# Mixer D's chunk recurrence for two pairs of heads at a time, and matmuls with 64 contraction rows in place of zero-padded ones

## Chip, cores and metric

One core of one Trainium2 chip runs the whole program in one launch. The metric is the time of that launch on the device in microseconds. TensorE is called PE here, VectorE DVE, ScalarE ACT, GpSimd POOL; SP issues the DMAs.

## What is computed

Two layers of a bidirectional encoder on 256 tokens of width 2048. Cut to what matters here:

```python
u = rmsnorm(h);  z = u @ w_in            # 6528 columns for the four mixers A, B, C, D
h += concat[A(zA), B(zB), C(zC), D(zD)] @ w_out
h += relu(rmsnorm(h) @ w_up)**2 @ w_down
h += (p @ w_ple) * sigmoid(rmsnorm(h) @ w_gate)
# A: 4 heads, two maps (m) of width 64 each, softmax(q k^T/8 + bias), o0 - lam*o1
# D (RWKV-7), 8 heads of width 64, forward and backward in time:
#   decay = exp(-0.607*sigmoid(w0 + tanh(wl) @ w2));  a = sigmoid(a0 + al @ a2);  g = sigmoid(gl) @ g2
#   state = state*w_t - (state @ kk_t) b_t^T + v_t k_t^T;   y_t = state @ r_t
#   out = (groupnorm(y) + bonus) * g
```

## The kernel before

Activations lie with the channel on the partition and the 256 tokens along the free axis. Every large product streams its weights from HBM in units of 128x1024 (512 KB). `wsplit` (L140) splits each unit into a rounded part `wh` (ACT, L148) and a remainder `wl` (DVE, L150), both `float32r`; `mm2` (L166, L167) or `mm3` (L158 to L160) multiplies them with the split activations `u`, `act`, `mh`. These rows are called weight rows below: an L166 row streams 512 columns, each of the others 256. The rest of the mixers' arithmetic is in plain `float32`, and PE runs such a matmul as two passes, each a record of the trace (a transpose is one).

Mixer D has two parts. `first` (L509, for c = 0 to 3, a pair of heads each) makes decay, rate and keys of a direction d, the products `psam` (L600) and transposed keys (`psbt`, L618). `invert` (L638) inverts small triangular blocks on DVE. `second` (L662) is called for c = 1, 3, 0, 2 one after the other (L439). In it `psW` (L704, L708) joins two 32-row blocks of each inverse, and four chunk steps follow, in each of which both directions advance by one chunk of 64 tokens: `psr`/`pss` gets the keys' product with the state (L741) and, from the step before, the values' part (`v_part`, L728); DVE copies it to `R` (L744); L749 multiplies it by the inverse; DVE copies that to `ST` (L751); L759 makes the state's increment; DVE multiplies the old state by the decay (L764) and adds (L768); L774 and L779 add to the output `psy`. Groupnorm and gating follow (L783 to L798).

`mixer_a` (L891) makes the logits of a head: two query blocks qc, two maps m. The query tile `qn` holds map 0 with its lower 64 rows zero and map 1 with its upper 64 rows zero (L910 to L912), so that L929 contracts over all 128 rows. In `first` the matrices of the decay and of the rate are laid out the same way: the tile `lora` holds 128 rows per direction, of which 64 are zero (L515, L556, L561).

No order is written out by hand: a scheduler places every engine's instructions when the program is built, from data dependencies and its own costs, so the steps of `second` stand between weight rows of the products that feed mixers A, B and C. Each engine then runs its list in that order. SBUF addresses come from pools; `shift` (L84) inserts a pad.

An operand's partitions set which part of PE's array a matmul takes: rows by where its inputs lie, columns by where its output lies in PSUM. L749 and L728 take 64 rows by 64 columns (L749 from partitions 0 to 63, L728 from 64 to 127, both to columns 0 to 63); L759 and L774 take all rows and, by turns, one or the other half of the columns; L600 by turns the upper and the lower half of the rows, and all columns.

Of the kernel before, what the change touches and what calls it, by code (L numbers as in the profile page):

```python
# [16 lines left out]
P = 128  # L17
# [17 lines left out]
PCOLS = [("mixg", 16), ("mlpg", 16), ("pleg", 16), ("aq", 2), ("ak", 1), ("asub", 1), ("hl0", 4), ("hl1", 4),  # L35
# [37 lines left out]
def trunk(ctx: ExitStack, tc: tile.TileContext, xT, pT, w_in, w_out1, w_out2, w_up, w_down, w_gate, w_ple, pvec,  # L73
          rel, lam, consts, lmask, onehot, lora, lorag, cw, outT, stages=None):
# [13 lines left out]
    shift(cp, 24)  # L88
# [180 lines left out]
    for l in range(DEPTH):  # L269
# [9 lines left out]
        mh1 = op_.__enter__().tile([P, NOUT1, 2 * S], F32R, name="mh1")  # L279
# [19 lines left out]
        for k in range(NOUT1):  # L299
            load_mix(mh1[:, k], k)  # L300
# [8 lines left out]
        mh2 = K.up.tile([P, KC - NOUT1, 2 * S], F32R, tag="u1", name="mh2")  # L309
        for k in range(NOUT1, KC):  # L310
            load_mix(mh2[:, k - NOUT1], k)
# [95 lines left out]
def mixers(K):  # L407
# [31 lines left out]
    for c in (1, 3, 0, 2):  # L439
        D.second(c)  # L440
# [14 lines left out]
class MixerD:  # L455
# [30 lines left out]
    def t2(self, tag="t2", bufs=4):  # L486
        return self.K.dp.tile([P, S], F32, tag=tag, name=tag, bufs=bufs)
# [21 lines left out]
    def first(self, c, base):  # L509
# [5 lines left out]
        lo = df.tile([P, 2, 2, P], F32, tag="lora", name="lora", bufs=1)  # L515
        nc.sync.dma_start(lo, K.lora[l, c])
        lg = df.tile([P, P], F32, tag="lorag", name="lorag", bufs=2)
        nc.sync.dma_start(lg, K.lorag[l, c])
# [29 lines left out]
        ksum = t1("ks", 1)  # L548
        for d in range(2):
            sd = sp[:, d]  # L550

            pad, inc0 = (0, 1) if d == 0 else (64, 0)
            sg = df.tile([P, 4, 65], F32, tag="sg", name="sg", bufs=1)
            V.memset(sg[:, :, pad:pad + 1], 0.0)
            ps = pds("psw")
            T.matmul(ps[:, :S], lo[:, 0, d], self.wl, start=True, stop=True)  # L556
            K.sigmoid(sg[:, :, inc0:inc0 + 64], ps[:, :S].rearrange("p (a b) -> p a b", a=4),
                      bias=self.nw[:, d * 4 + c:d * 4 + c + 1])
            a = t1()
# [48 lines left out]
            for blk in range(2):  # L608
# [4 lines left out]
            BE = df.tile([P, 3, P], F32, tag="BE", name="BE", bufs=1)  # L613
            G.tensor_tensor(BE, BK[:, d:d + 3].rearrange("p j a b -> p j (a b)"),
                            EL[:, d:d + 3].unsqueeze(2).to_broadcast([P, 3, P]), ALU.mult)
            ps = pds("psbt")
            for j in range(3):
                T.transpose(ps[:, j * P:(j + 1) * P], BE[:, j], mat("ident"))  # L618
# [14 lines left out]
        T.matmul(ps[:, :S], lg, self.gl, start=True, stop=True)  # L633
# [28 lines left out]
    def second(self, c):  # L662

        K, t2, sp, xs = self.K, self.t2, self.sp.pop(c), self.xs
        if c == 0:
            sp = self.slot(c)
            for d in range(2):
                K.nc.sync.dma_start(sp[:, d], self.sscr[c, d])
        nc, l, dp = K.nc, K.l, K.dp
        V, A, G, T = nc.vector, nc.scalar, nc.gpsimd, nc.tensor  # L670
        mat, pc, pds = K.mat, K.pc, K.pds


        ST = dp.tile([P, 2, 4, 2, 64], F32, tag="ST", name="ST", bufs=1)
        for d in range(2):
            nc.sync.dma_start(ST[64:, d].rearrange("p j h v -> p j (h v)"),
                              self.vscr[c].rearrange("(j s) v -> s j v", s=64))

        def am(rows, d, h, j, a):
            o = SP_AM + h * 512 + j * P + a * 64  # L680
            return sp[rows, d, o:o + 64]

        TT = dp.tile([P, 2, 8, 64], F32, tag="lane", name="Tm", bufs=2)

        U = dp.tile([P, 8, 32], F32, tag="U32", name="U32", bufs=2)
        W = dp.tile([P, 8, 32], F32, tag="W32", name="W", bufs=1)
        G.memset(TT[0:64], 0.0)
        bs = [slice(0, 32), slice(32, 64)]

        def v8(t):  # L690
            return t.rearrange("p (a b) -> p a b", a=8)
        for d in range(2):
            lane = (d * 64 + c * 16) * 1024
            Tm = TT[:, d]

            x, y = (0, 1) if d == 0 else (1, 0)
            for t, b, w in ((U[bs[x]], x, d), (Tm[bs[0], :, bs[0]], 0, 1 - d), (Tm[bs[1], :, bs[1]], 1, 1 - d)):
                nc.sync.dma_start(t, bass.AP(xs.tensor, xs.offset + w * P * 1024 + lane + b * 8192,
                                             [[32, 32], [1024, 8], [1, 32]]))

            ps = pds("psW")
            for i in range(8):
                o = SP_AM + i * P
                T.matmul(ps[bs[y], i * 32:(i + 1) * 32], sp[bs[x], d, o + 32 * y:o + 32 * y + 32], U[bs[x], i],  # L704
                         start=True, stop=True)
            A.activation(W[bs[y]], v8(ps[bs[y], :S]), AF.Copy)
            for i in range(8):
                T.matmul(ps[bs[x], S + i * 32:S + (i + 1) * 32], W[bs[y], i], Tm[bs[y], i, bs[y]],  # L708
                         start=True, stop=True)
            V.tensor_copy(Tm[bs[x], :, bs[y]], v8(ps[bs[x], S:]))  # L710


        SS = dp.tile([P, 3, 2, P], F32, tag="SS", name="SS", bufs=1)
        G.memset(SS, 0.0)

# [3 lines left out]
        def both(ap, o, w):  # L719

            return strided(ap, o(0), [[o(1) - o(0), 2], [1, w]])

        def v_part(ps, st):
            for d in range(2):
                j = at(st, d)
                for h in range(2):
                    o = S + d * P + h * 64
                    T.matmul(ps[0:64, o:o + 64], am(slice(64, P), d, h, j, 0), ST[64:, d, j, h],  # L728
                             start=(st == 0 and d + h == 0), stop=(st == 0), skip_group_check=True)
        psr = pds("psr")  # L730
        v_part(psr, 0)
        bg = dp.tile([P, 2, S], F32, tag="bg2", name="bg2", bufs=2)
        nc.sync.dma_start(bg, self.late[c])
        psy = pds("psy")
        first = [True, True]
        for st in range(4):
            js = [at(st, d) for d in range(2)]
            if st:
                for d in range(2):
                    o = SP_KS + js[d] * P  # L740
                    T.matmul(psr[0:64, S + d * P:S + (d + 1) * P], sp[:, d, o:o + 64], SS[:, st - 1, d],  # L741
                             start=False, stop=True, skip_group_check=True)
            R = dp.tile([P, 2, P], F32, tag="R", name="R", bufs=1)
            V.tensor_copy(R[0:64], psr[0:64, S:].rearrange("p (a b) -> p a b", a=2))  # L744
            psr = pds("pss")
            for d in range(2):
                for h in range(2):
                    o = d * P + h * 64
                    T.matmul(psr[0:64, o:o + 64], TT[0:64, d, h * 4 + js[d]], R[0:64, d, h * 64:(h + 1) * 64],  # L749
                             start=(d + h == 0), stop=True, skip_group_check=True)  # L750
            V.tensor_copy(both(ST[0:64], lambda d: d * 512 + js[d] * P, P),  # L751
                          psr[0:64, :S].rearrange("p (a b) -> p a b", a=2))
            if st < 3:
                v_part(psr, st + 1)
                ps = pds("psst")
                for d in range(2):
                    o = SP_BB + (js[d] - d) * P
                    for h in range(2):
                        T.matmul(ps[HS[h], d * 64:d * 64 + 64], sp[:, d, o:o + P][:, HS[h]], ST[:, d, js[d], h],  # L759
                                 start=True, stop=True)  # L760
                pst = ps[:, :P].rearrange("p (a b) -> p a b", a=2)
                if st:
                    dec = dp.tile([P, 2, P], F32, tag="dec", name="dec", bufs=1)
                    V.tensor_tensor(dec, SS[:, st - 1], strided(sp, SP_EL + js[0], [[SP_N + js[1] - js[0], 2], [0, P]]),  # L764
                                    ALU.mult)
                for h in range(2):
                    if st:
                        V.tensor_tensor(SS[HS[h], st, :, HS[h]], dec[HS[h], :, HS[h]], pst[HS[h]], ALU.add)  # L768
                    else:
                        V.tensor_copy(SS[HS[h], st, :, HS[h]], pst[HS[h]])  # L770
# [417 lines left out]
```

## Time and profile before

| | us |
|---|---|
| median of 3 runs | 2740.97 (2737.82 to 2740.99) |
| the profiled execution | 2741.71 |
| its span, first to last instruction | 2740.0 |
| PE busy | 2688.3 (98%) |
| DVE busy | 1972.6 (72%) |
| ACT busy | 1608.3 (59%) |
| POOL busy | 77.3 (3%) |

The profiled execution lies 0.74 us above the median. Busy time counts a matmul until its modelled end, and matmuls overlap, so a row's start and the start of the next row tell what it took of PE. Mixer D of layer 0 runs from the start to about 460 us, beside A, B and C from about 145 us; layer 1's mixers lie between about 1300 and 1860 us; what is left is the large products alone.

### The profile page before, as it was taken

The page shows a single profiled execution, that of the slowest core. Times are in us where ns is not written, and L with a number is a line of the kernel's source. Part 1 is how long each engine was busy: PE and PEld are TensorE (multiplying, and loading weights), DVE is VectorE, ACT ScalarE, POOL GpSimd, SP SyncE. Part 2 cuts the span into 40 slices and gives each one's busy share as a digit, 9 for nine tenths or more (in the row PEclk, how much of TensorE's full clock was granted, in tenths as well). Part 3 has the DMA queues.
Part 4 walks back from the last instruction along what each step waited for, and adds up shares of the span by engine and source line. Part 5 has one row for each costly group of instructions (what it writes and reads, how often), then busy time and mean ns, then how long its engine had stood idle before and what let it go on. Part 6 is the DMA issues. An engine that isn't in the chain of part 4 may idle for free.

```text
span 2740.0 us, 47071 instructions
## 1 busy us (share of the span) xinstructions
PE 2688.3 (98%) x17014; PEld 2356.8 (86%) x17014; DVE 1972.6 (72%) x4025; ACT 1608.3 (59%) x3254; POOL 77.3 (3%) x106
## 2 busy tenths in 40 slices
PE   8999999999999999999999999999999999999999
PEld 7877888898888888888898778888888888888888
DVE  7888767686666666677878877677766666666776
ACT  6755555476645546456767655555665465564565
POOL 0001010000000000000001001000000000000000
PEclk9999999999999999999999999999999999999999
DMA  6645454665555555556556444545655555555565
GB/s 221 200 153 156 133 162 153 211 198 191 190 190 189 192 189 188 192 190 196 177 183 190 155 150 135 179 126 188 201 192 190 188 191 192 187 190 192 187 202 162
DMA packets 186402, 496.76 MB, mean 181 GB/s; under 512 B 46996, under 2 KB 66068, under 8 KB 186040
## 3 DMA queue, kind: packets, MB, share of 16 engines
q1 hardware_dynamic: 186168, 493.76, 55.7%
q8 instruction: 133, 2.18, 0.3%
q14 instruction: 101, 0.83, 0.1%
HBM read 474.01 MB, written 19.68 MB: 180 GB/s over the span
## 4 chain that ended last, share of the span: by engine, by line
PE 87%; DVE 4%; DMA 4%; ACT 3%; issue 1%; SPq 0%; DVEq 0%; ACTq 0%
PE acc L166 48%; PE acc L167 25%; PE acc L160 2%; PE acc L158 2%; PE acc L159 2%; DVE wl L150 1%; ACT wh L148 1%; PE psbl L1019 1%; DMA ot<-o_scr 1%; PE pss L749 1%; DMA sp<-s_scr 1%; PE psy L779 1%; PE psam L600 1%; PE pss L728 1%; PE pss L741 0%
## 5 line engine op out<-in xcount | busy, mean ns | idle before, releaser
L148 ACT ACTIVATE wh<-raw 128x512 fp32r<-128x512 f32 x1704 | 1074.3, 631 | 963.7 <-PE acc L166 631.0
L150 DVE TENSOR_TENSOR wl<-raw,wh 128x512 fp32r<-128x512 f32 x1704 | 1176.1, 691 | 623.9 <-ACT wh L148 612.0
L166 PE MATMUL acc<-u,wh 128*128 128x512 f32 x3200 | 1143.1, 398 | 3.4 <-DVE z L240 2.7
L167 PE MATMUL acc<-u,wl 128*128 128x256 f32 x3200 | 914.9, 286 | 8.3 <-DVE wl L150 8.0
L166 PEld LDWEIGHTS acc<-u,wh 128*128 128x128 f32 x3200 | 602.5, 188 | 134.9 <-DVE z L240 3.1
L166 PE MATMUL acc<-act,wh 128*128 128x512 f32 x2048 | 710.2, 390 | 0.0
L167 PEld LDWEIGHTS acc<-u,wl 128*128 128x128 f32 x3200 | 603.9, 189 | 21.9 <-DVE wl L150 14.5
L167 PE MATMUL acc<-act,wl 128*128 128x256 f32 x2048 | 577.5, 282 | 0.0
L166 PEld LDWEIGHTS acc<-act,wh 128*128 128x128 f32 x2048 | 384.3, 188 | 80.6
L167 PEld LDWEIGHTS acc<-act,wl 128*128 128x128 f32 x2048 | 387.1, 189 | 0.0
L166 PE MATMUL acc<-ug,wh 128*128 128x512 f32 x512 | 179.4, 393 | 0.0
L158 PE MATMUL acc<-u,wh 128*128 128x256 f32 x480 | 141.5, 295 | 9.8 <-ACT u L191 8.2
L160 PE MATMUL acc<-u,wl 128*128 128x256 f32 x480 | 142.6, 297 | 6.4 <-DVE wl L150 6.3
L167 PE MATMUL acc<-ug,wl 128*128 128x256 f32 x512 | 143.0, 281 | 0.0
L166 PE MATMUL acc<-mh,wh 128*128 128x512 f32 x384 | 138.3, 401 | 3.2 <-ACT wh L148 2.6
L159 PE MATMUL acc<-u,wh 128*128 128x256 f32 x480 | 139.2, 290 | 0.8 <-DVE u L192 0.6
L166 PEld LDWEIGHTS acc<-ug,wh 128*128 128x128 f32 x512 | 95.8, 188 | 19.4
L167 PE MATMUL acc<-mh,wl 128*128 128x256 f32 x384 | 109.7, 287 | 1.8 <-DVE wl L150 1.8
L160 PEld LDWEIGHTS acc<-u,wl 128*128 128x128 f32 x480 | 92.7, 193 | 12.6 <-DVE wl L150 9.9
L158 PEld LDWEIGHTS acc<-u,wh 128*128 128x128 f32 x480 | 92.8, 193 | 11.4 <-ACT u L191 8.4
L167 PEld LDWEIGHTS acc<-ug,wl 128*128 128x128 f32 x512 | 96.4, 188 | 0.9
L159 PEld LDWEIGHTS acc<-u,wh 128*128 128x128 f32 x480 | 92.8, 193 | 2.5 <-DVE u L192 1.7
(305 smaller groups left out, 2670.6 us busy)
## 6 DMA issues: line engine op xcount, KB each, us to landing
raw<-in_w_up SPq DMA_DIRECT2D x256, 512.0 KB
raw<-in_w_down SPq DMA_DIRECT2D x256, 512.0 KB
raw<-in_w_in SPq DMA_DIRECT2D x204, 512.0 KB
raw<-in_w_gate SPq DMA_DIRECT2D x64, 512.0 KB
raw<-in_w_out SPq DMA_DIRECT2D x32, 512.0 KB
raw<-in_w_out SPq DMA_DIRECT2D x64, 256.0 KB
h<-in_xT SPq DMA_DIRECT2D x8, 512.0 KB
ot<-o_scr SPq DMA_DIRECT2D x32, 128.0 KB
```

Of the source, the lines that this page charges most:

```text
L148: A.activation(wh[:, :n], raw[:, o:o + n], AF.Copy)
L150: V.tensor_tensor(wl[:, :n], raw[:, o:o + n], wh[:, :n].bitcast(F32), ALU.subtract)
L158: T.matmul(ps[:, :S], w1, act[:, :S], start=start, stop=False)
L159: T.matmul(ps[:, :S], w1, act[:, S:], start=False, stop=False)
L160: T.matmul(ps[:, :S], w2, act[:, :S], start=False, stop=stop)
L166: T.matmul(ps, wh[:, b * P:(b + 1) * P], act, start=start, stop=False)
L167: T.matmul(ps[:, :S], wl[:, b * P:(b + 1) * P], act[:, :S], start=False, stop=stop)
L600: T.matmul(pm[h][:, j * P:(j + 1) * P], BK[HS[h], j].rearrange("p a b -> p (a b)"), KS[HS[h], j].rearrange("p a b -> p (a b)"), start=True ...
L728: T.matmul(ps[0:64, o:o + 64], am(slice(64, P), d, h, j, 0), ST[64:, d, j, h], start=(st == 0 and d + h == 0), stop=(st == 0), skip_group_ ...
L749: T.matmul(psr[0:64, o:o + 64], TT[0:64, d, h * 4 + js[d]], R[0:64, d, h * 64:(h + 1) * 64], start=(d + h == 0), stop=True, skip_group_che ...
L779: T.matmul(psy[:, j * 64:(j + 1) * 64], SS[:, st - 1, d], sp[:, d, o:o + 64], start=False, stop=True, skip_group_check=True)
L1019: T.matmul(p2[:, i * P:(i + 1) * P], kc[:, i * P:(i + 1) * P], strided(Q, i * P, [[2 * hh, P // (2 * hh)], [W + hh, 2], [1, hh]]), start=T ...
```

## The change

- `second` is called for two c at once: (1, 3), then (0, 2). Its tiles are twice as large and lie in a new pool `d2`; copies of the first c of the two go to DVE, those of the second to ACT.
- In a chunk step the L749 products alternate with the next step's `v_part`, which now goes to another PSUM bank (L773 and L741 of the new file). `psW` products of the two directions are written by turns (L718, L724).
- The transposed keys are no longer multiplied by the chunk's decay on POOL (`BE` goes); the state is multiplied by it after the increment is added: on DVE for the first c, on ACT for the second.
- Matrices of decay, rate and gate come in one DMA for each c, without zeros; L557 contracts 64 rows for each direction. `mixer_a` makes one query tile and contracts 64 rows for each map (L958).
- `mh1` becomes 12 tiles, and the pad ahead of the constants is 32 bytes shorter, so what lies behind it in the left part of SBUF moves down by 32 bytes.

```diff
-    for c in (1, 3, 0, 2):
-        D.second(c)
+    d2_ = tc.tile_pool(name="d2", bufs=1, side="right", reuse_waits="tile")
+    K.d2 = d2_.__enter__()
+    for cs in ((1, 3), (0, 2)):
+        D.second(cs)
...
-        lo = df.tile([P, 2, 2, P], F32, tag="lora", name="lora", bufs=1)
+        lo = df.tile([P, 3, P], F32, tag="lora", name="lora", bufs=2)
...
+        for x, act in ((0, self.wl), (1, self.al)):
+            pws = [pds("psw") for _ in range(2)]
+            for d in range(2):
+                T.matmul(pws[d][:, :S], lo[HS[d], x, :], act[HS[d], :], start=True, stop=True)
...
-            T.matmul(ps[:, :S], lo[:, 0, d], self.wl, start=True, stop=True)
...
-            BE = df.tile([P, 3, P], F32, tag="BE", name="BE", bufs=1)
-            G.tensor_tensor(BE, BK[:, d:d + 3].rearrange("p j a b -> p j (a b)"),
-                            EL[:, d:d + 3].unsqueeze(2).to_broadcast([P, 3, P]), ALU.mult)
...
             for i in range(8):
-                T.matmul(ps[bs[x], S + i * 32:S + (i + 1) * 32], W[bs[y], i], Tm[bs[y], i, bs[y]],
-                         start=True, stop=True)
+                for d, (x, y) in enumerate(xy):
+                    T.matmul(pw[d][bs[x], S + i * 32:S + (i + 1) * 32], W[bs[y], i], Tm[bs[y], d, i, bs[y]],
+                             start=True, stop=True)
...
+            pss, psr = pds("pss"), pds("psr") if st < 3 else None
+            for p, d, h in PDH:
+                o = (p * 2 + d) * P + h * 64
+                T.matmul(pss[0:64, o:o + 64], TT[p][0:64, d, h * 4 + js[d]], R[0:64, p, d * P + h * 64:d * P + (h + 1) * 64],
+                         start=(p + d + h == 0), stop=True, skip_group_check=True)
+                if st < 3:
+                    v_part(psr, st + 1, p, d, h)
...
+                for p, d, h in PDH:
+                    o, q = SP_BB + (js[d] - d) * P, (p * 2 + d) * 64
+                    T.matmul(ps[HS[h], q:q + 64], sps[p][:, d, o:o + P][:, HS[h]], ST[:, p, d, js[d], h],
+                             start=True, stop=True)
...
+                V.tensor_tensor(SS[:, st, 0], SS[:, st, 0],
+                                strided(sps[0], SP_EL + js[0], [[SP_N + js[1] - js[0], 2], [0, P]]), ALU.mult)
                 for d in range(2):
+                    o = SP_EL + js[d]
+                    A.activation(SS[:, st, 1, d], SS[:, st, 1, d], AF.Identity, scale=sps[1][:, d, o:o + 1])
...
-            qn = ab.tile([P, 2, S], F32, tag="bQ", name="qn")
-            for m in range(2):
-                V.scalar_tensor_tensor(qn[:, m], t, pc(l, gn, m), rs, ALU.mult, ALU.mult)
...
+        pls = [K.pab("psl") for _ in range(2)]
         for m in range(2):
-            pl = K.pab("psl")
-            T.matmul(pl[:, :S], qn[:, m, qs], kn, start=True, stop=True)
+            T.matmul(pls[m][:, :S], qn[HS[m], qs], kn[HS[m], :], start=True, stop=True)
```

PE's list in one chunk step of `second`, layer 0 (`pss`: the inverse's products, `psr`: keys and values, `psst`: the state's increment, `psy`: the output, `sp`: what `first` left for a c). Before, for c = 1:

```order
L749 MATMUL pss<-R,Tm 64x64 x4
...
L728 MATMUL pss<-ST,sp_1065 64x64 x4
L759 MATMUL psst<-ST,sp_1065 64x64 x4
L774 MATMUL psy<-sp_1065,ST 64x64 x2
L779 MATMUL psy<-sp_1065,SS 128x64
L774 MATMUL psy<-sp_1065,ST 64x64 x2
L779 MATMUL psy<-sp_1065,SS 128x64
```

With the change, the first step for c = 1 and 3 (the first two rows stand eight times in all, one after the other):

```order
L773 MATMUL pss<-R,Tm 64x64
L741 MATMUL psr<-ST,sp_1057 64x64
...
L785 MATMUL psst<-ST,sp_1057 64x64 x4
L785 MATMUL psst<-ST,sp_1770 64x64 x4
L802 MATMUL psy<-sp_1057,ST 64x64 x4
L802 MATMUL psy<-sp_1770,ST 64x64 x4
L166 MATMUL acc<-u_104,wh 128x512
...
L764 MATMUL psr<-SS,sp_1057 64x128 x2
L764 MATMUL psr<-SS,sp_1770 64x128 x2
```

The value products, which stood in a run of their own, now stand one by one between the inverse's products, and runs of two c stand together; 16 weight rows lie between L802 and L764.

The same list in `mixer_a`, the first head's second query block (`psl`: logits), with the change:

```order
L972 MATMUL psct<-cst,L 128x128 x2
L958 MATMUL psl<-x_2825,x_2760 128x256
L167 MATMUL acc<-u_104,wl 128x256
...
L166 MATMUL acc<-u_104,wh 128x512
L958 MATMUL psl<-x_2825,x_2760 128x256
L167 MATMUL acc<-u_104,wl 128x256
```

The products of the two maps stand eight weight rows apart, as L929's did before; of the 32 L958 products 30 stand alone and two stand together.

In `first`, with the change (`psw`: decay from `wl`, rate from `al`):

```order
L541 MATMUL psvt<-cst,v 128x128 x2
L557 MATMUL psw<-wl,lora 128x256 x2
L557 MATMUL psw<-al,lora 128x256
L160 MATMUL acc<-u_104,wl 128x256
...
L557 MATMUL psw<-al,lora 128x256
L160 MATMUL acc<-u_104,wl 128x256
```

Three of the four L557 products of a c stand together, and the fourth alone; before there were L556 and L561 for one direction here and for the other some 60 rows on.

## Rows read from the trace of the kernel before

**Rows 1.** Page: busy time by engine; the ending chain by engine.

```profile
PE 2688.3 (98%) x17014; PEld 2356.8 (86%) x17014; DVE 1972.6 (72%) x4025; ACT 1608.3 (59%) x3254; POOL 77.3 (3%) x106
...
PE 87%; DVE 4%; DMA 4%; ACT 3%; issue 1%; SPq 0%; DVEq 0%; ACTq 0%
```

**Rows 2.** Stretches: PE, PEld, DVE, ACT, POOL busy us (x), PEclk, DMA share, GB/s.

```profile
200.00:250.00 50.00, 47.41 (x280) 40.00 (x279) 46.80 (x116) 29.68 (x67) 7.99 (x11) 1.00 0.55 170
...
300.00:350.00 50.00, 50.00 (x409) 41.35 (x408) 36.56 (x80) 25.96 (x61) 6.23 (x11) 1.00 0.43 133
```

**Rows 3.** Waits of PE: us in total, times, longest us.

```profile
PE acc L167 <- DVE wl L150: 9.8, 18, 1.9
...
PE psam L600 <- DVE BK L593: 3.4, 4, 0.9
...
PE psW L704 <- DMA U<-x_scr: 1.9, 2, 1.2
```

**Rows 4.** Timeline, PE, chunk step of c = 1, layer 0: start us, us to modelled end.

```profile
278.38 0.28 PE L167 MATMUL acc<-u,wl 128*128 128x256 f32 x1
278.50 0.39 PE L166 MATMUL acc<-u,wh 128*128 128x512 f32 x1
278.73 0.28 PE L167 MATMUL acc<-u,wl 128*128 128x256 f32 x1
278.94 0.68 PE L749 MATMUL pss<-R,Tm 64*64 64x64 f32 x8
279.54 0.50 PE L166 MATMUL acc<-u,wh 128*128 128x512 f32 x1
...
282.05 0.67 PE L728 MATMUL pss<-ST,sp 64*64 64x64 f32 x8
282.66 0.45 PE L759 MATMUL psst<-ST,sp 128*64 128x64 f32 x8
282.94 0.29 PE L774 MATMUL psy<-sp,ST 128*64 128x64 f32 x4
283.15 0.43 PE L779 MATMUL psy<-sp,SS 128*128 128x64 f32 x2
283.52 0.34 PE L774 MATMUL psy<-sp,ST 128*64 128x64 f32 x4
283.79 0.43 PE L779 MATMUL psy<-sp,SS 128*128 128x64 f32 x2
284.03 0.36 PE L167 MATMUL acc<-u,wl 128*128 128x256 f32 x1
...
287.42 0.65 PE L741 MATMUL pss<-SS,sp 128*64 128x128 f32 x4
288.00 0.50 PE L166 MATMUL acc<-u,wh 128*128 128x512 f32 x1
```

**Rows 5.** Timeline, PE, `psam` of `first` by turns on two halves of the rows.

```profile
63.21 1.16 PE L600 MATMUL psam<-sp,BK 64*128 64x128 f32 x16
64.30 0.39 PE L160 MATMUL acc<-u,wl 128*128 128x256 f32 x1
```

**Rows 6.** Timeline, PE, one zero-padded logits product of `mixer_a`.

```profile
258.05 0.59 PE L929 MATMUL psl<-x,qn 128*128 128x256 f32 x2
258.29 0.47 PE L167 MATMUL acc<-u,wl 128*128 128x256 f32 x1
258.60 0.39 PE L166 MATMUL acc<-u,wh 128*128 128x512 f32 x1
```

**Rows 7.** Timeline, PE, eight `psW` products of one direction.

```profile
248.13 0.69 PE L704 MATMUL psW<-U,sp 32*32 32x32 f32 x16 [1.17 <-DMA U<-x_scr]
248.75 0.50 PE L166 MATMUL acc<-u,wh 128*128 128x512 f32 x1
```

**Rows 8.** Groups by line, DVE, shapes apart: the state's update. Count, busy us, mean ns.

```profile
L768 DVE TENSOR_TENSOR SS<-dec,psst 64x128 f32<-64x128 f32 x32 | 9.1, 283 | 3.2 <-PE psst L759 2.8
...
L764 DVE TENSOR_TENSOR dec<-SS,sp 128x256 f32<-128x256 f32 x16 | 6.7, 421 | 0.2
```

More of the change, by code (lines that the diff above doesn't have):

```diff
@@ L278, in trunk @@
         op_ = tc.tile_pool(name="op", bufs=1, side="right", reuse_waits="tile")
-        mh1 = op_.__enter__().tile([P, NOUT1, 2 * S], F32R, name="mh1")
+        opool = op_.__enter__()
+        mh1 = [opool.tile([P, 2 * S], F32R, tag="mh%d" % k, name="mh1") for k in range(NOUT1)]
         def load_mix(dst, k):
@@ L299, in trunk @@
         for k in range(NOUT1):
-            load_mix(mh1[:, k], k)
+            load_mix(mh1[k], k)
         for m in range(KC):
@@ L309, in trunk @@
         mh2 = K.up.tile([P, KC - NOUT1, 2 * S], F32R, tag="u1", name="mh2")
+        mh2 = [mh2[:, k] for k in range(KC - NOUT1)]
         for k in range(NOUT1, KC):
-            load_mix(mh2[:, k - NOUT1], k)
+            load_mix(mh2[k - NOUT1], k)
         pgw = wide.enter_context(tc.tile_pool(name="pgw", bufs=4, space=PSUM, reuse_waits="tile"))
@@ L660, in invert, with second @@
             nc.sync.dma_start(self.xs[y], t)
[L662 to L669, printed above, removed]
+    def second(self, cs):
+        K, t2, xs = self.K, self.t2, self.xs
+        nc, l, dp, d2 = K.nc, K.l, K.dp, K.d2
         V, A, G, T = nc.vector, nc.scalar, nc.gpsimd, nc.tensor
@@ L685, in second @@
-        U = dp.tile([P, 8, 32], F32, tag="U32", name="U32", bufs=2)
-        W = dp.tile([P, 8, 32], F32, tag="W32", name="W", bufs=1)
-        G.memset(TT[0:64], 0.0)
+        sps = []
+        for c in cs:
+            sp = self.sp.pop(c)
+            if c == 0:
+                sp = self.slot(c)
+                for d in range(2):
+                    nc.sync.dma_start(sp[:, d], self.sscr[c, d])
+            sps.append(sp)
+        ST = d2.tile([P, 2, 2, 4, 2, 64], F32, tag="ST", name="ST", bufs=1)
@@ L688, in second, with am @@
+        for p, c in enumerate(cs):
+            for d in range(2):
+                nc.sync.dma_start(ST[64:, p, d].rearrange("p j h v -> p j (h v)"),
+                                  self.vscr[c].rearrange("(j s) v -> s j v", s=64))
+        def am(rows, p, d, h, j, a):
+            o = SP_AM + h * 512 + j * P + a * 64
+            return sps[p][rows, d, o:o + 64]
         bs = [slice(0, 32), slice(32, 64)]
+        xy = [(0, 1), (1, 0)]
         def v8(t):
             return t.rearrange("p (a b) -> p a b", a=8)
[L692 to L701, printed above, removed]
-            for i in range(8):
-                o = SP_AM + i * P
-                T.matmul(ps[bs[y], i * 32:(i + 1) * 32], sp[bs[x], d, o + 32 * y:o + 32 * y + 32], U[bs[x], i],
-                         start=True, stop=True)
-            A.activation(W[bs[y]], v8(ps[bs[y], :S]), AF.Copy)
-            for i in range(8):
-                T.matmul(ps[bs[x], S + i * 32:S + (i + 1) * 32], W[bs[y], i], Tm[bs[y], i, bs[y]],
-                         start=True, stop=True)
-            V.tensor_copy(Tm[bs[x], :, bs[y]], v8(ps[bs[x], S:]))
@@ L714, in second @@
+        SS = d2.tile([P, 3, 2, 2, P], F32, tag="SS", name="SS", bufs=1)
         G.memset(SS, 0.0)
+        PD = [(p, d) for p in range(2) for d in range(2)]
+        PDH = [(p, d, h) for p, d in PD for h in range(2)]
         def at(st, d):
             return st if d == 0 else 3 - st
[L719 to L729, printed above, removed]
@@ L734, in second, with copy @@
+        bgs = []
+        for c in cs:
+            bg = dp.tile([P, 2, S], F32, tag="bg2", name="bg2", bufs=2)
+            nc.sync.dma_start(bg, self.late[c])
+            bgs.append(bg)
         psy = pds("psy")
         first = [True, True]
+        def copy(p, dst, src):
+            if p == 0:
+                V.tensor_copy(dst, src)
+            else:
+                A.activation(dst, src, AF.Copy)
         for st in range(4):
@@ L738, in second @@
             if st:
-                for d in range(2):
[L740 to L770, printed above, removed]
@@ L771, in second @@
-            for d in range(2):
-                j = js[d]
-                for h in range(2):
-                    T.matmul(psy[HS[h], j * 64:(j + 1) * 64], ST[:, d, j, h], am(slice(0, P), d, h, j, 1),
-                             start=first[h], stop=False, skip_group_check=True)
-                    first[h] = False
-                if st:
-                    o = SP_KS + j * P + 64
-                    T.matmul(psy[:, j * 64:(j + 1) * 64], SS[:, st - 1, d], sp[:, d, o:o + 64], start=False,
-                             stop=True, skip_group_check=True)
+                for p, d in PD:
+                    o, q = SP_KS + js[d] * P, (p * 2 + d) * P
+                    T.matmul(psr[0:64, q:q + P], sps[p][:, d, o:o + 64], SS[:, st - 1, p, d],
+                             start=False, stop=True, skip_group_check=True)
@@ new lines, in second @@
+            for p, d, h in PDH:
+                j = js[d]
+                T.matmul(psy[HS[h], p * S + j * 64:p * S + (j + 1) * 64], ST[:, p, d, j, h], am(slice(0, P), p, d, h, j, 1),
+                         start=first[h], stop=False, skip_group_check=True)
+                first[h] = False
+            for p, d in PD if st else []:
+                j = js[d]
+                o = SP_KS + j * P + 64
+                T.matmul(psy[:, p * S + j * 64:p * S + (j + 1) * 64], SS[:, st - 1, p, d], sps[p][:, d, o:o + 64],
+                         start=False, stop=True, skip_group_check=True)
@@ L801, in prepare @@
+        V.tensor_tensor(flat(y), flat(y), flat(rs), ALU.mult)
+        for p, c in enumerate(cs):
+            A.activation(y[:, p], y[:, p], AF.Identity, scale=pc(l, "gng", c), bias=pc(l, "gnb", c))
+            V.tensor_tensor(y[:, p], y[:, p], bgs[p][:, 0], ALU.add)
+            V.tensor_tensor(y[:, p], y[:, p], bgs[p][:, 1], ALU.mult)
+            K.put(12 + c, y[:, p])
 def prepare(K):
```

141 lines of the change are left out of this document (84 added, 57 removed).

## Prediction

> **What bounds the kernel now.** I read the page first: PE is busy for 98% of the span and carries 87% of the chain that ended last [rows 1]. A busy PE need not be a useful one, so next I read the stretches. From 300 to 350 us, in the middle of mixer D's second half, PE is never idle, while DVE is busy for 36.6 of 50 us and ACT for 26.0; from 200 to 250 us DVE is at 46.8 of 50 [rows 2], which is `invert` beside the first head's mixers. The list of PE's waits says how much is left for other engines to give: the largest group, for `wl`, is 9.8 us in 18 waits over the whole run [rows 3]. So in `second` the time is what PE's list costs, record after record, and the question is what a record costs from its start to the next start. That I read in the timeline.
>
> **Prices.** A weight row of 256 columns takes 0.12 us and one of 512 columns 0.23 us (278.38, 278.50, 278.73) [rows 4].
> - *64 columns, one array part.* L749's eight passes run 278.94 to 279.54, L728's 282.05 to 282.66 [rows 4]: 0.60 to 0.61 us.
> - *64 columns, two parts by turns.* L759's eight passes, on alternate halves of the columns, take 0.28 us (282.66 to 282.94) [rows 4], half as long. A pass alone is thus worth 0.0585 us and so are two that share: 4 x 0.0585 = 0.23, and 0.05 for the first, whose second half can't be prepared ahead. L749 is then 0.05 + 8 x 0.0585 + 0.08.
> - *Entering and leaving an array shape.* L749 starts 0.21 after an L167 that is worth 0.12, so entering costs 0.09; the 0.08 above is the price of leaving, taken as 0.09. The Trainium skill, TensorEngine Tiling (Array Packing), Key Properties, says that a change of tiling mode drains the engine; the trace agrees, with these 0.09 us each way.
> - *128 columns.* L741's four passes take 0.58 us (287.42 to 288.00) [rows 4]: 4 x 0.11 + 0.05 + 0.09. L600's sixteen, by turns on two halves of the rows, take 1.09 us (63.21 to 64.30) [rows 5]; alone they would take 16 x 0.11 = 1.76. So halves of the rows share as halves of the columns do: 8 x 0.11 = 0.88, and 0.21 for the first pass and leaving.
> - *256 columns.* L929 takes two passes from 258.05 to 258.60, less the 0.12 of the L167 between: 0.43 us [rows 6].
>
> **The recurrence.** Before, for one c: four L749 runs of 0.09 + 0.60 = 2.76; the steps with L779 (two), 0.09 + (284.03 - 282.05) = 2.07 each, 4.14; the first step, without L779, 0.09 + 0.61 + 0.28 + 0.33 = 1.31; the last, without L728 and L759, 0.09 + 0.05 + (284.03 - 282.94) = 1.23; three L741 runs, 3 x 0.67 = 2.01. Sum 11.45 us, 22.9 for two c.
>
> With the change, for two c: three runs of 32 passes in 16 shared places, 0.09 + 0.05 + 16 x 0.0585 + 0.09 = 1.17 each, 3.5; the last step's L773 has no partner and takes 16 places too, 1.17; the first L785 and L802, 32 passes in 16 places, 1.17. Where L808 follows, its eight passes don't share: 0.09 for the shape, 0.16 for the first (283.15 to 283.52 holds such a one), then about 0.11 each as for L741, 0.93 + 0.09; two steps of 2.1 and the last 1.6. L764 takes 0.09 + 0.05 + 8 x 0.11 + 0.09 = 1.10, three times 3.3. Sum 14.9. The gain is 8.0 us for two c, and there are four such calls in both layers: **-32 us**. Bounds: if L808's passes take 0.16 each, 3.6 us less; if the alternate row halves didn't share, 3 x 16 x 0.0585 x 4 = 11 us less.
>
> **psW.** Sixteen passes take 0.62 us (248.13 to 248.75), less 0.12 for first and leaving 0.032 each [rows 7]; 512 of them are 16.4 us. If every one shared, 8.2 would go; in the new order most eights of one direction still stand behind one another, and only some go by turns. I take **-3** (0 to -8). The value products ahead of the first step lose a switch: -0.6.
>
> **The half products.** Here the order decides. An L958 or L557 that shares saves 0.43 us; one that stands alone still takes its two passes of 0.215, and enters and leaves an array shape that the weight rows around it don't have: 0.09, and 0.21 as for L600, is **0.30 more** than L929 costs now. Thirty L958 and eight L557 stand alone: +11.4. One pair and eight runs of three share: 0.43 - 0.30 = 0.13 each, -1.2. Together **+10**. The Trainium skill, TensorEngine Tiling (Array Packing), Theoretical Speedup, gives up to twice the speed for 64 contraction rows; no lone one can have that, and by it the 64 products would give 13.8 us where I charge 10.
>
> **What I cost at nothing.** POOL's multiplication goes: PE waits for POOL nowhere in its list of waits. The transposes' order, the 12 tiles of `mh1` and eight DMA issues fewer on SP change no row that PE waits for. DVE and ACT: two copies and the decay move to ACT, busy for 26 of 50 us in that stretch [rows 2]; cover is what stands on PE between. The reload of c = 0 waits on SP's queue for the end of c = 3 as before, and holds the weight loads behind it as before. The shorter pad shifts `wh`, `wl` and `u`; no row tells of a price of addresses. In `first` both directions' chains now stand 24 weight rows (2.9 us) apart where there were 52; DVE is near its limit there, and PE waited for BK four times for 3.4 us in all [rows 3]. I take waits as unchanged, with +8 us at the upper end (1 us for each of eight c) and -4 at the lower, since waits like the 1.17 for U [rows 7] come once for two c.
>
> **Sum.** -32 - 3 - 0.6 + 10 = -25 us. Against the execution's own 2741.7 us that is 2716.7; it lies 0.7 above the median of the runs. I forecast **2717 us**.
>
> **Rivals.**
> 1. *Slower: the step's chain on DVE and ACT outlasts its cover.* The decay used to be multiplied beside PE's work; now increment, decay and the next L764 follow one another: two additions (0.28 each for 128 columns, more for the 256 now) and a product of 0.42 [rows 8], about 1.5 us with the half on ACT. L802 and 16 weight rows cover 0.57 + 8 x 0.35 = 3.4 us. Twelve such steps would have to lose 2.6 us each to eat 25 us and 6 more; so it decides only if the chain takes 6 us, four times its work, by queueing behind `wh` and `wl`. At 3 us each: 2753. For it: the chain is longer and crosses engines. Against: neither is full there [rows 2]. 5%.
> 2. *The alternate row halves don't share,* since L773 and L741 both write columns 0 to 63 of their banks. Against: L600's halves both write all columns [rows 5]. 2717 + 11 = 2728. 6%.
> 3. *Same: first's chains and the half products take all of it.* DVE stays the limit in `first` and `invert`, and PE's gain in `second` is met by new waits of 1 to 2 us a step: 2717 + 12 x 2 = 2741. For it: mixer B's levels lose the recurrence's rows that stood between them, and DVE works steadily there. 7%.
> 4. *The halves share although the list parts them,* by the page's rule above: if neither alone nor in turn a switch were paid, 2717 - 10 - 14 = 2693. Against: the 0.09 us at every change of shape [rows 4]. 3%.
>
> **How the numbers follow.** The main case has 79%. Its own bounds are L808 (+4), psW (+3, -5), waits (+8, -4): not all at once, 2706 to 2730. The range reaches to rival 2 with a little of the waits on top, and down to cheaper half products: 2704 to 2733. Left out are rivals 1, 3 and 4 and the main case's tails, just under 2 in 10. A measurement of this kernel can tell about 0.2% from no change, 5.5 us. Faster by more: the main case, rivals 2 and 4, 88%; within: rival 3, 7%; slower: rival 1, 5%.
>
> **What would show each step right or wrong.** In the changed profile: L773 and L741 in one stretch, 32 passes in about 1.1 us; L785 with L802 the same; L764's eight passes in 1.0; a lone L958 that takes about 0.3 us longer between weight rows than L929's 0.43; waits of PE for `wl`, BK and L764's operands no longer in total than now, and the stretches from 600 us on of the same length. I am wrong if the alternating run takes 2 us, if PE waits ahead of L764 or L773 at every step, or if lone half products cost what L929 did.

## The result, and the profile after

The changed kernel takes 2705.35 us (median of four runs, 2701.65 to 2707.77); the kernel before took 2740.98 beside it. The ratio is 0.9872, with a 95% interval of 0.9854 to 0.9890: 35 us faster. The forecast was 2717 us with a range of 2704 to 2733. The profiled execution took 2701.65 us, its span is 2699.6; it is the fastest of the four.

The page of the changed kernel: PE's row, and the shares of the chain that ended last, by engine.

```profile
PE 2652.9 (98%) x16998; PEld 2323.8 (86%) x16998; DVE 1944.9 (72%) x3949; ACT 1618.1 (60%) x3294; POOL 59.9 (2%) x86
...
PE 89%; DVE 5%; DMA 3%; ACT 2%; issue 1%; POOL 1%; SPq 0%; DVEq 0%; POOLq 0%; ACTq 0%
```

PE is still the bound, as in [rows 1], and has lost 35.4 us of busy time. The table by stretch of the changed kernel, for two stretches inside mixer D's second half, shows that the two copies and the decay which moved to ACT leave PE no idle time there: PE is busy throughout, DVE is at 32 to 34 of 50 us and ACT at 28 to 29, where [rows 2] had 36.6 and 26.0.

```profile
250.00:300.00 50.00, 50.00 (x461) 41.96 (x461) 32.05 (x73) 29.48 (x69) 1.84 (x2) 0.98 0.34 104
300.00:350.00 50.00, 50.00 (x505) 41.40 (x506) 34.43 (x73) 28.16 (x63) 5.81 (x10) 1.00 0.56 177
```

PE's list of waits in the changed kernel (waited for, total us, times, longest), the answer to [rows 3]:

```profile
PE acc L167 <- DVE wl L150: 10.1, 17, 3.1
PE acc L158 <- ACT u L191: 9.2, 2, 8.8
PE acc L160 <- DVE wl L150: 7.3, 9, 1.0
PE psc L918 <- POOL zd L916: 2.8, 2, 1.4
...
PE psam L609 <- DVE BK L602: 1.5, 6, 0.3
...
PE psW L718 <- DMA U<-x_scr: 1.0, 3, 0.5
```

No wait of a chunk step is in it. BK went from 3.4 to 1.5 us; one for POOL is new. All rows of the list together make 45.0 us before and 39.3 now. This total is that of one execution and not firm: it is 44.5 in `e1_pad24` (below), whose engines have the same lists as the changed kernel.

Where the time went can be read by counting weight rows: at the 450th L166 or L158 the changed kernel is 3.5 us ahead, at the 900th 20.2, then 20.2 up to the 3300th, and 40.3 from the 4500th to the end. All of it lies in the two layers' mixers, half in each; the large products between are the same to 0.1 us.

PE's timeline of the changed kernel (start, length, engine, line) for an alternating run of 32 passes, its first and last rows; then a step's increments and outputs, then L764:

```profile
264.91 0.27 PE L773 MATMUL pss<-R,Tm 64*64 64x64 f32 x1
264.92 0.27 PE L741 MATMUL psr<-ST,sp 64*64 64x64 f32 x1
...
265.84 0.22 PE L773 MATMUL pss<-R,Tm 64*64 64x64 f32 x1
265.84 0.22 PE L741 MATMUL psr<-ST,sp 64*64 64x64 f32 x1
265.99 0.48 PE L976 MATMUL pso<-ct,x 128*128 128x256 f32 x1
```

```profile
269.60 0.69 PE L785 MATMUL psst<-ST,sp 128*64 128x64 f32 x16
270.11 0.64 PE L802 MATMUL psy<-sp,ST 128*64 128x64 f32 x16
270.68 1.11 PE L808 MATMUL psy<-sp,SS 128*128 128x64 f32 x8
271.62 0.65 PE L982 MATMUL psan<-t,cst 128*128 128x256 f32 x2
```

```profile
274.98 1.09 PE L764 MATMUL psr<-SS,sp 128*64 128x128 f32 x8
275.99 0.50 PE L166 MATMUL acc<-u,wh 128*128 128x512 f32 x1
```

The 32 alternating passes take 1.08 us (264.91 to 265.99), L785 with L802 also 1.08, L808 0.94, L764 1.01. L773 and L741 start within 0.01 us of each other, 16 times: the halves of the rows share.

### The profile page after: what moved, and what is told of

The parts are those of the page before. It is cut to its first block, busy times and chain, and to the rows that moved or that the text cites. A ratio compares the mean times of both kernels' runs of the same rounds, so it can differ in the third digit from the quotient of the medians.

```text
span 2699.6 us, 46908 instructions
## 1 busy us (share of the span) xinstructions
PE 2652.9 (98%) x16998; PEld 2323.8 (86%) x16998; DVE 1944.9 (72%) x3949; ACT 1618.1 (60%) x3294; POOL 59.9 (2%) x86
## 4 chain that ended last, share of the span: by engine, by line
PE 89%; DVE 5%; DMA 3%; ACT 2%; issue 1%; POOL 1%; SPq 0%; DVEq 0%; POOLq 0%; ACTq 0%
PE acc L166 49%; PE acc L167 26%; PE acc L160 3%; PE acc L158 2%; PE acc L159 2%; DVE wl L150 2%; PE psl L958 1%; PE psbl L1050 1%; PE pss L773 1%; PE psam L609 1%; PE psr L764 0%; PE psy L808 0%; ACT wh L148 0%; DMA ot<-o_scr 0%; DMA raw<-in_w_out 0%
## 5 line engine op out<-in xcount | busy, mean ns | idle before, releaser
L166 PE MATMUL acc<-u,wh 128*128 128x512 f32 x3200 | 1135.6, 397 | 2.4 <-ACT wh L148 2.4
L167 PE MATMUL acc<-u,wl 128*128 128x256 f32 x3200 | 909.5, 285 | 10.0 <-DVE wl L150 9.7
L166 PEld LDWEIGHTS acc<-u,wh 128*128 128x128 f32 x3200 | 602.1, 188 | 136.7 <-ACT wh L148 6.6
L166 PE MATMUL acc<-act,wh 128*128 128x512 f32 x2048 | 710.2, 390 | 0.0
L167 PEld LDWEIGHTS acc<-u,wl 128*128 128x128 f32 x3200 | 603.6, 189 | 28.4 <-DVE wl L150 19.1
L167 PE MATMUL acc<-act,wl 128*128 128x256 f32 x2048 | 577.6, 282 | 0.0
L166 PEld LDWEIGHTS acc<-act,wh 128*128 128x128 f32 x2048 | 384.4, 188 | 80.5
L167 PEld LDWEIGHTS acc<-act,wl 128*128 128x128 f32 x2048 | 387.4, 189 | 0.0
L166 PE MATMUL acc<-ug,wh 128*128 128x512 f32 x512 | 179.4, 393 | 0.0
L158 PE MATMUL acc<-u,wh 128*128 128x256 f32 x480 | 138.0, 288 | 10.9 <-ACT u L191 9.2
L160 PE MATMUL acc<-u,wl 128*128 128x256 f32 x480 | 140.2, 292 | 7.3 <-DVE wl L150 7.3
L167 PE MATMUL acc<-ug,wl 128*128 128x256 f32 x512 | 143.1, 281 | 0.0
L166 PE MATMUL acc<-mh,wh 128*128 128x512 f32 x384 | 135.9, 394 | 0.8 <-DVE h L171 0.7
L166 PEld LDWEIGHTS acc<-ug,wh 128*128 128x128 f32 x512 | 95.9, 188 | 19.4
L167 PE MATMUL acc<-mh,wl 128*128 128x256 f32 x384 | 110.6, 289 | 0.7 <-DVE wl L150 0.4
L160 PEld LDWEIGHTS acc<-u,wl 128*128 128x128 f32 x480 | 91.6, 191 | 14.1 <-DVE wl L150 11.1
L158 PEld LDWEIGHTS acc<-u,wh 128*128 128x128 f32 x480 | 91.8, 191 | 12.3 <-ACT u L191 9.4
L167 PEld LDWEIGHTS acc<-ug,wl 128*128 128x128 f32 x512 | 96.5, 188 | 0.9
```

The source lines that it names most:

```text
L158: T.matmul(ps[:, :S], w1, act[:, :S], start=start, stop=False)
L160: T.matmul(ps[:, :S], w2, act[:, :S], start=False, stop=stop)
L166: T.matmul(ps, wh[:, b * P:(b + 1) * P], act, start=start, stop=False)
L167: T.matmul(ps[:, :S], wl[:, b * P:(b + 1) * P], act[:, :S], start=False, stop=stop)
```

## The experiments

Each was timed against the kernel before; differences between kernels are taken from the ratios, with 0.1% as 2.74 us. A ratio's interval reaches about 0.15% to either side, so a difference of two can be told from zero from about 6 us on.

### Is it the addresses? (pads)

The weight rows had become shorter although nothing in them was changed. Between starts, a row of L158 to L160 took 119.5 ns on average before and 117.0 with the change, L166 and L167 together (a pair) 349.7 and 347.9 in the mixers, 346.8 in both in the long products. Theory A below puts this down to the pad, which moves operands by 32 bytes. In `e1_pad24` the changed kernel gets `shift(cp, 24)` again, in `e2_before_pad16` the kernel before gets `shift(cp, 16)`; each engine's list stays as it was. (The change also takes one column for each layer, `aq`, from the table of constants, 8 bytes in all, which `e1_pad24` does not give back.)

> The changed kernel with the pad ahead of the constants back at 24 columns: every engine's list is the same, only what lies behind the pad in the left part of SBUF is 32 bytes higher. Theory A (addresses set what a weight row takes: rows of mm3 go from 119.5 to 116.9 ns with the change, L166 in the mixers from 232.7 to 230.1): both means return to the values of before, 2016 x 2.6 ns = 5.2 us and some 1900 x 1.9 ns = 3.6 us, so about 9 us slower than the changed kernel, 2714. Theory B (the unpredicted part of the gain is fewer waits of PE): no difference, 2705, and rows of mm3 stay at 117.

> The kernel before with the pad at 16 columns, nothing else: all lists as before. Theory A (addresses): rows of mm3 fall to 117 ns and the time to 2741 - 9 = 2732. Theory B (waits): 2741, rows of mm3 stay at 119.5.

`e2_before_pad16`: 0.9971 (0.9962 to 0.9981), 8 us faster than before. `e1_pad24`: 0.9896 (0.9879 to 0.9913), 6.6 us slower than the changed kernel, just at the edge of what can be told. The rows themselves are clearer. Layer 0 has one unbroken run of 192 rows of mm3; its first and last row on PE's timeline, before, with the change, and in both experiments:

```profile
542.80 0.28 PE L158 MATMUL acc<-mh,wh 128*128 128x256 f32 x1
...
565.71 0.28 PE L160 MATMUL acc<-mh,wl 128*128 128x256 f32 x1
```

```profile
523.25 0.28 PE L158 MATMUL acc<-mh,wh 128*128 128x256 f32 x1
...
545.54 0.28 PE L160 MATMUL acc<-mh,wl 128*128 128x256 f32 x1
```

```profile
529.51 0.28 PE L158 MATMUL acc<-mh,wh 128*128 128x256 f32 x1
...
552.43 0.28 PE L160 MATMUL acc<-mh,wl 128*128 128x256 f32 x1
```

```profile
537.89 0.28 PE L158 MATMUL acc<-mh,wh 128*128 128x256 f32 x1
...
560.18 0.28 PE L160 MATMUL acc<-mh,wl 128*128 128x256 f32 x1
```

Over 191 steps 22.91 us before and 22.92 in `e1_pad24`, 22.29 with the change and in `e2_before_pad16`: 119.9 ns with 24 columns of pad, 116.7 with 16, whatever else the kernel does. Over all of them `e2_before_pad16` has 117.2 ns for a row of mm3 and 348.0 for the mixers' pair: 2016 rows by 2.3 ns and 1536 pairs by 1.7 are 7.2 of the 8 us measured. Theory A holds.

Two more look for the rule, both on `e3_full_logits` (below): `e9_weights_moved` has `shift(wp, 16)` for `shift(wp, 24)`, `e10_pad8` has `shift(cp, 8)` for `shift(cp, 16)`.

> e3_full_logits with the second pad, the one ahead of the weight tiles, 8 columns shorter: wh and wl lie 32 bytes lower and the activations u where they were; all lists the same. Theory U (the address of the activations that a row streams sets its time): rows of mm3 stay at 117 ns, the time at 2688 to 2690. Theory W (the address of the weights, or where weights and activations lie to one another): rows of mm3 at 119 to 120 ns, some 8 us slower, 2697.

> e3_full_logits with the first pad at 8 columns: all that lies behind it is 32 bytes lower than there and 64 lower than with 24 columns; all lists the same. Theory (what counts is the place within 64 bytes): rows of mm3 back at 119.5 ns, as with 24 columns, and 8 to 9 us slower than with 16, 2697. Rival (the lower the better, or only the one place of before is bad): 117 ns and 2688 to 2690.

`e9_weights_moved`: 0.9891 (0.9876 to 0.9905), 23 us slower than `e3_full_logits`. `e10_pad8`: 0.9834 (0.9817 to 0.9850), 7 us slower. Neither went by the theories' rows. In `e9_weights_moved` the run of 192 rows (starts at 516.47 to 538.97) takes 117.8 ns a row, but the pair L166 and L167 takes 350.1 ns in the long products and 351.6 in the mixers: 3.3 and 3.6 ns for 6144 pairs are 21 us. In `e10_pad8` that run (519.84 to 542.34) takes 117.8 too, the long products stay at 346.8, and only the mixers' pair rises, to 351.5. So it isn't the place within 64 bytes.

The kernel's pools fit a simple reading. The mixers' activations lie in the right part of SBUF, where no pad moves them, so both experiments put the weights 64 bytes lower against them than the kernel before has them, and the mixers' rows come out alike. In the long products, `u` lies behind the first pad and ahead of the second: `e10_pad8` moves it along with the weights, and its pair stays; `e9_weights_moved` moves the weights alone, and its pair goes to 352.7, while the pairs of `act`, which lies behind both pads, stay at 346.7. So how weights and activations lie to one another decides, and not the place of either alone. Why a distance is good or bad for a product stays open.

### What do the half products cost?

In `e3_full_logits` the changed kernel gets mixer A's zero-padded query tile back; in `e4_full_both` also zero-padded matrices of decay and rate, five blocks for each c. `e8_before_half_logits` is the kernel before with mixer A's edit alone.

```diff
-            T.matmul(pls[m][:, :S], qn[HS[m], qs], kn[HS[m], :], start=True, stop=True)
+            T.matmul(pls[m][:, :S], qn[:, m, qs], kn, start=True, stop=True)
```

```diff
-                T.matmul(pws[d][:, :S], lo[HS[d], x, :], act[HS[d], :], start=True, stop=True)
+                T.matmul(pws[d][:, :S], lo[:, x * 2 + d, :], act, start=True, stop=True)
```

> The changed kernel with mixer_a's query tile zero-padded again, so that the logits contract 128 rows. The theory of the prediction (a lone half-array product costs 0.30 us more than a full one, a shared one 0.13 less): 30 x 0.30 less 0.26, so 8.7 us faster than the changed kernel, 2696.5. Rival (the added time of a half product is hidden, since the weight rows behind it are ready sooner or PE waits less): within 3 us of 2705.

> The changed kernel with the logits and the matrices of decay and rate zero-padded. The theory of the prediction: 10 us faster than the changed kernel, 2695, of which about 1.4 is due to decay and rate. Rival: within 3 us of 2705. A second rival for the second part alone: the zero-padded matrices cost 2.5 times 64 KB more DMA for each c at the start, where the DMA queues are full, and give the 1.4 back.

> The kernel before with mixer_a's logits contracted over 64 rows, nothing else; 24 of the products stand alone, four pairs side by side. Theory 1 (a lone one costs 0.30 us more, one that shares 0.13 less): 7.2 - 1.0 = 6 us slower than before, 2747. Theory 2 (beside that, a lone half-array product makes TensorE's granted clock fall near it, as it falls at 240 us of the changed kernel and not where the logits contract 128 rows): 10 to 16 us slower, 2751 to 2757, and a mean granted clock 0.002 lower. Rival (half products cost what full ones did): 2741.

`e3_full_logits`: 2687.98 us, 0.9807 (0.9794 to 0.9820), 18 us faster than the changed kernel. `e4_full_both`: 2689.82 us, 0.9812 (0.9799 to 0.9825); decay and rate make no difference that can be told. `e8_before_half_logits`: 1.0039 (1.0026 to 1.0052), 11 us slower than before, as its second theory said. All three lie beyond the price of the prediction. Addresses, which these edits move by the 8 bytes of `aq`, are not the reason: rows of mm3 and pairs take 117.0, 348.0 and 346.8 ns in `e3_full_logits`, as in the changed kernel, and in `e8_before_half_logits` the mixers' pair alone rises, by 0.9 ns, 1.4 us in all. So first that price. PE's timeline of the changed kernel, a lone L958:

```profile
256.97 0.28 PE L167 MATMUL acc<-u,wl 128*128 128x256 f32 x1
257.18 0.70 PE L958 MATMUL psl<-x,x 64*128 64x256 f32 x2
257.80 0.28 PE L785 MATMUL psst<-ST,sp 128*64 128x64 f32 x2
```

L167 is worth 0.12, so the entry costs 0.09; the two passes and the exit take 0.62, together 0.71 against 0.43 in [rows 6]: 0.28 more, where 0.30 was charged. The price is right; something comes on top. It is in the clock column (the first number behind POOL's count) of the tables by stretch, of the changed kernel, of `e3_full_logits` and of `e8_before_half_logits`:

```profile
235.00:240.00 5.00, 4.50 (x69) 3.61 (x67) 2.46 (x5) 3.66 (x8) 0.57 (x1) 1.00 0.64 134
240.00:245.00 5.00, 5.00 (x76) 3.59 (x74) 2.00 (x5) 0.37 (x1) 0.00 (x0) 0.65 0.61 158
245.00:250.00 5.00, 5.00 (x36) 4.53 (x34) 2.42 (x7) 2.11 (x7) 0.00 (x0) 0.50 0.46 140
250.00:255.00 5.00, 5.00 (x48) 3.80 (x48) 2.79 (x6) 2.05 (x5) 0.00 (x0) 0.83 0.10 13
```

```profile
240.00:245.00 5.00, 5.00 (x84) 4.39 (x83) 2.30 (x5) 2.77 (x6) 0.00 (x0) 1.00 0.83 216
245.00:250.00 5.00, 5.00 (x78) 4.13 (x78) 3.77 (x11) 2.39 (x7) 0.00 (x0) 1.00 0.54 151
```

```profile
250.00:255.00 5.00, 4.63 (x50) 3.64 (x51) 1.85 (x4) 0.76 (x2) 0.00 (x0) 0.83 0.71 184
255.00:260.00 5.00, 5.00 (x29) 3.23 (x28) 1.26 (x3) 0.79 (x2) 0.00 (x0) 0.50 0.17 66
260.00:265.00 5.00, 5.00 (x25) 3.81 (x25) 3.05 (x8) 3.64 (x11) 0.00 (x0) 0.65 0.12 25
```

In the changed kernel the granted clock stands at half, 1.2 GHz, for some 10 us around 246: (1 - 0.65) x 5 + (1 - 0.50) x 5 + (1 - 0.83) x 5 = 5.1 us are lost. PE's timeline of that stretch:

```profile
238.41 1.09 PE L718 MATMUL psW<-U,sp 32*32 32x32 f32 x32
...
240.85 0.57 PE L724 MATMUL psW<-Tm,W 32*32 32x32 f32 x13
241.35 1.14 PE L958 MATMUL psl<-x,x 64*128 64x256 f32 x2
242.42 1.06 PE L724 MATMUL psW<-Tm,W 32*32 32x32 f32 x16
243.41 1.22 PE L958 MATMUL psl<-x,x 64*128 64x256 f32 x2
244.56 1.05 PE L724 MATMUL psW<-Tm,W 32*32 32x32 f32 x16
245.54 1.97 PE L741 MATMUL psr<-ST,sp 64*64 64x64 f32 x16
247.44 0.58 PE L167 MATMUL acc<-u,wl 128*128 128x256 f32 x1
```

From 238.4 to 247.4 PE had nothing but small and half-array products; L958 took 1.07 us (241.35 to 242.42) instead of 0.62, and the clock came back after 4 us of weight rows. The dip at this place stands in the profiles of all seven kernels with half-array logits (the changed one, `e1`, `e5` to `e8`, `e11`) and in none of the seven without; `e1_pad24` and `e7_psw_runs` show another in layer 1, of 17 and 10 us. Over all runs the mean clock was 0.9950 with the change and 0.9980 in `e3_full_logits`: 0.0030 x 2705 = 8.1 us, an estimate, since a run's clock is on record to 0.001. With the 8.7 us of the price that makes 16.8 of the 18 measured. In the same way `e8_before_half_logits` had 0.9950 against 0.9968 before, 4.9 us, and with 6.2 of the price 11.1, near the 10.7 measured. So half-array logits bring the dip; what in them lowers the clock is not settled: `e3_full_logits` also has weight rows among its psW products, and PE idled 0.5 us ahead of the fall in the changed kernel, and 2.4 us from 245 to 255 in `e8_before_half_logits`, against 1.9 before.

### What do alternation and pairing bring?

`e5_values_apart` writes the values' part behind the inverse products, `e6_one_c` calls `second` for one c after another, `e7_psw_runs` puts d outside i in psW's loops; all three on the changed kernel.

```diff
-                if st < 3:
-                    v_part(psr, st + 1, p, d, h)
+            for p, d, h in PDH if st < 3 else []:
+                v_part(psr, st + 1, p, d, h)
```

```diff
-    for cs in ((1, 3), (0, 2)):
+    for cs in ((1,), (3,), (0,), (2,)):
```

> The changed kernel with the values' part (L741) written behind the eight inverse products (L773) of a step in place of between them; on PE's list they now stand in runs of 4 or 8 of one kind. Theory (halves of the rows share the array when they alternate): in each of 12 steps 32 passes need 32 places of 0.0585 us in place of 16, 12 x 0.94 = 11.2 us, a little less where runs of four touch; 11 us slower than the changed kernel, 2716. Rival (a pass costs half as much only because two c stand together): 2705.

> The changed kernel with the second half called for one c after another: the alternation stays, the pairing goes (the decay of every c is multiplied on DVE). Theory (prices of the prediction): for one c 3 x 0.70 for alternating runs, 0.70 for the last inverse products, 0.70 + 2 x 1.28 + 0.9 for increments and outputs, 3 x 0.67 for L764, together 9.0 us, where two c at once cost 14.9: 8 x (9.0 - 7.45) = 12 us slower than the changed kernel, 2717, so that alternation alone is worth 20 of the 32 us. Rival A (the pairing is worth nothing, since waits of the longer chains take its gain): 2705. Rival B (the pairing carries nearly all): 2730.

> The changed kernel with the small products that join the inverse's blocks written as eights of one direction again. Theory (by turns they share the array): 3 us slower, 2708. Rival (they do not share, or the time there is set by something else): 2705.

`e5_values_apart`: 0.9900 (0.9886 to 0.9913), 7.7 us slower than the changed kernel. PE's timeline, one step:

```profile
255.32 0.97 PE L773 MATMUL pss<-R,Tm 64*64 64x64 f32 x13
256.08 0.27 PE L741 MATMUL psr<-ST,sp 64*64 64x64 f32 x1
...
256.18 0.22 PE L741 MATMUL psr<-ST,sp 64*64 64x64 f32 x1
256.19 0.22 PE L773 MATMUL pss<-R,Tm 64*64 64x64 f32 x1
...
256.30 0.92 PE L741 MATMUL psr<-ST,sp 64*64 64x64 f32 x13
257.15 0.44 PE L972 MATMUL psct<-cst,L 128*128 128x128 f32 x2
```

The same 32 passes take 1.83 us and not 1.08; three pairs at the seam still start together. Other steps mix more (1.47 us at 268.6), and the twelve together take 7.5 us more than in the changed kernel, hence 7.7 and not 11.2. Sharing is shown, and the rival, that pairing alone halves a pass, falls.

`e6_one_c`: 0.9906 (0.9891 to 0.9921), 9 us slower, where 12 were expected. Pairing is real, and alternation without it keeps the larger part. `e7_psw_runs`: 0.9888 (0.9874 to 0.9901), 4 us slower where 3 were expected; that is less than can be told from zero, so this is not shown.

### Did the decay's move cost nothing?

`e11_decay_on_keys` (on the changed kernel) and `e12_full_logits_decay_on_keys` (on `e3_full_logits`) multiply the keys by the decay on POOL again, and the old state beside PE's work.

```diff
+            BE = df.tile([P, 3, P], F32, tag="BE", name="BE", bufs=1)
+            G.tensor_tensor(BE, BK[:, d:d + 3].rearrange("p j a b -> p j (a b)"),
+                            EL[:, d:d + 3].unsqueeze(2).to_broadcast([P, 3, P]), ALU.mult)
...
-                V.tensor_tensor(SS[:, st, 0], SS[:, st, 0],
-                                strided(sps[0], SP_EL + js[0], [[SP_N + js[1] - js[0], 2], [0, P]]), ALU.mult)
+                    V.tensor_tensor(dec[:, 0], SS[:, st - 1, 0],
+                                    strided(sps[0], SP_EL + js[0], [[SP_N + js[1] - js[0], 2], [0, P]]), ALU.mult)
```

> The changed kernel with the decay where it was: POOL multiplies the transposed keys by it (BE), and the old state is multiplied beside PE's work, on DVE for the first c and on ACT for the second. Theory (the step's chain on DVE and ACT is covered, and BE is off PE's path): within 3 us of the changed kernel, ratio to before 0.987. Rival A (dropping BE is what shortened PE's waits for BK and the lanes' tiles in the first part, 45 to 39 us in all): 5 us slower, PE's wait for BK back at 3 us. Rival B (the decay behind the addition holds L764 up): 3 to 10 us faster.

> e3_full_logits with the same edit, logits over 128 rows. Theory: as e3_full_logits, ratio to before 0.981, 2687 where before is 2740, and a mean granted clock of 0.998, since no lone half-array logits stand beside the second half. Rival A: 5 us slower. Rival B: 3 to 10 us faster, the fastest of all.

0.9899 (0.9885 to 0.9913) and 0.9825 (0.9811 to 0.9838): 7 and 5 us slower than their bases, the one just above and the other just below what can be told, both to the same side. PE's waits in `e11_decay_on_keys`:

```profile
PE psW L721 <- DMA U<-x_scr: 4.2, 3, 2.2
PE psc L923 <- POOL zd L921: 4.1, 2, 2.0
PE psam L609 <- DVE BK L602: 3.2, 6, 0.5
```

The wait for BK is back at 3.2 us (in `e12_full_logits_decay_on_keys` too), as in [rows 3], and the whole list at 46.8 against 39.3; at the 300th weight row, in `first`, the kernel is already 4.1 us behind. Rival A holds for this wait: dropping BE shortened it, in a part that I had charged nothing. It is 1.7 us of the 7; of the rest no cause is shown. In `e12_full_logits_decay_on_keys` the whole list is no longer than in its base (37.9 against 42.2), and the profiled execution is no slower (2690.83 against 2693.46), so what its 5 us are, if they are real, stays open. Rival B, that the longer chain holds L764 up, falls: neither is faster without that chain.

## Why the prediction was right, and where not

- **The recurrence, -32 us: right.** Each run came out as priced: 1.08 us for 32 shared passes (1.17 with the 0.09 of entering), 0.94 for L808, 1.01 for L764. From start to next start the rows L728 to L779 took 89.7 us before, L741 to L808 take 62.5 now; entering them cost 8.4 and costs 4.0: -31.6.
- **psW, -3: not shown** in size. Its rows fell by 1.6 us, and 1 us of what they still take is due to the dip of the clock; only a few passes of a run stand by turns.
- **The half products, +10: mis-sized.** The price of a lone one was right, 0.28 for 0.30. Left out was the clock: with half-array logits it falls beside psW, and restoring them brought 18 us, not 8.7. By the Trainium skill, TensorEngine Tiling (Array Packing), Theoretical Speedup, 64 contraction rows may be up to twice as fast. The trace agrees where two halves alternate (1.08 against 1.83 us) and disagrees where one stands alone (0.71 with entry and exit against 0.43).
- **The shorter pad, "no row tells of a price of addresses": this step failed.** It was 8 us of gain, shown by `e2_before_pad16`. Rows of the trace before did hold it: a row of mm3 took 119.9 ns and L167, with as many columns, 116 to 118.
- **Waits unchanged, +8 to -4: near.** They fell by 5.7 us in the profiled executions; 1.9 of it is the wait for BK, 3.2 to 3.5 us in all five kernels with BE and 1.0 to 1.5 in the nine without. The rest is not firm, as the 44.5 us of `e1_pad24` show.
- **The rivals.** That DVE and ACT outlast their cover, that row halves don't share, that waits eat the gain, that lone halves cost no switch: each falls, by the waits above, `e5_values_apart`, the result, and L958's 0.71 us.

With what the runs show, the sum is -32 (recurrence) - 2 (psW and values) + 10 (lone halves) + 4 (clock, 0.9965 before and 0.9950 now) - 6 (waits) - 8 (addresses) = -34, against -35.6 in the medians. The waits' term is the loose one, and about 2 us of the dip stand both in the first two terms and in the clock's. The forecast's -25 was short by addresses and waits, and the clock hid some of that. That 2705 still fell inside the range, 1.4 us above its lower end, is partly luck: the 8 us of addresses, for which no bound stood, nearly took it out, and the 4 us of the clock, which stood in no term either, held it in.

The fastest version is `e3_full_logits`: paired heads and alternating halves, but full-array logits, 2687.98 us, 53 us below the kernel before and 18 below the change.

## What to carry to other kernels

In this kernel half-array products paid only where the list of the engine, not the source, put their partners beside them; look there, and try zero-padding what stands alone. When a change moves what lies in SBUF, compare the start-to-start time of the rows that it didn't touch: 2 ns on some 3500 rows and pairs are worth 8 us here, a quarter of what the rewritten loop brings. And read the clock column beside every stretch that became dense with small products.

## What the runs showed of the hardware

Where operands lie in SBUF moves a float32r matmul of 256 columns between 116.7 and 119.9 ns, and a pair of 512 and 256 columns between 346.8 and 350.1 in the long products and between 347.9 and 351.6 in the mixers, with no list changed; 32 bytes suffice, and which products lose depends on which block of tiles is moved. Passes on the two halves of the rows share the array though both take the same half of its columns (L773 and L741 both write to partitions 0 to 63): 32 passes of 64 columns in 1.08 us. They do so even where the list has them in runs, for the few passes at the seam.
